# A top-k search tied to token tiles and matrix products, instead of running freely between two fixed pauses

## The chip, the cores and the metric

The kernel runs on one core of a Trainium2 chip. The metric is device time in microseconds (us) of one execution; lower is better. The engines named below are TensorE (PE; its weight loads are a row of their own, PEld), VectorE (DVE), ScalarE (ACT) and GpSimd (POOL); SyncE (SP) issues DMAs. Each engine works through its own instructions in one fixed order and waits at an instruction until its inputs and its buffers are ready.

## The reference, cut to what matters

The kernel computes one transformer layer for 1024 tokens of width 1024. The combined projection `h @ w_in` feeds an indexed sparse attention, a retention and two gates; then come an output projection and a gated feed-forward part.

```python
h = _rmsnorm(x, norm1_w) * (1.0 + scale1) + shift1
qa, ka, va, iq, ik, iw, qr, kr, vr, gr, ga, gb = split(h @ w_in)
# sparse attention: per query the 256 keys with the highest index score
score = einsum('bqh,bqhs->bqs', iw * w_scale, relu(einsum('bqhd,bsd->bqhs', iq, ik) * idx_scale))
_, idx = lax.top_k(where(causal, score, NEG), topk)
y_a = attention(qa, ka[idx], va[idx]) @ w_attn_proj
# retention: 4 heads, chunks of 128 tokens, a state r carried from chunk to chunk
ret = _retention(rotate(qr), rotate(kr), vr)
y_r = (silu(gr) * _head_groupnorm(ret, gn_w)) @ w_ret_proj
merged = sigmoid(ga) * y_a + sigmoid(gb) * y_r
```

## The kernel before

**Matrix products.** A float32 product is made of three passes on TensorE over operands split into a high and a low part (`whi`, `wlo`; `hT_hi`, `hT_lo`). ACT writes the high part of a weight (L77, L750), and the low part, the weight minus its high part, is a subtraction on POOL (L80, L751).

**Stages that the change touches, in order of time.** Times are of the profiled execution.
- About 128 to 238 us: the projection for the attention's values (`V`, 192 matmuls over 8 token tiles) with the index scores woven in. `score_units` makes the scores of query blocks 2 to 7 in units: four transposes (L414) and a split on DVE (`qst`, L417) per half of the heads, then per unit two matmuls (L424, L425), a ReLU on ACT (L428) and a multiply-add on DVE (L430, L432). A linear rule `n` of the step number says from which V step a unit comes after.
- 238 to 484 us: the retention in two pairs of heads (`hp` 0 and 1). Each pair has a Q/K projection with a rotation on POOL (L657), and then a loop over eight token tiles that makes V, the masked `inn` (a multiply on DVE, L675) and, one tile later, `chunk`: output, state `rst` (DVE, L694) and the statistics `bn_stats`, `bn_aggr` (DVE, L700, L701). During `hp` 0 `mod_work` computes the modulation vector from streamed weights (`macc`, DVE). During `hp` 1 `add_up` (L621, L623) forms `S1`, a sum of token halves of `h`; ScalarE and DVE split it (L633).
- 499 to 770 us: the gates and the attention's Q and K by a Strassen-like scheme: 13 streams of weight columns (`flow`), 7 products each (`M1` to `M7`, of 12 matmuls), 91 in all. The list `seq` sets their order; the first two streams alternate. `M5`, `M6`, `M3` and `M7` need the token sums `S1`, `S2`, `S4` and `S3`, which DVE forms and splits (L621, L623, L633); it also forms sums of weight blocks (`wraw`, L789, L796) and adds products (L810). `S3` is written over one of `h`'s own halves.
- 740 to 863 us: `make_g`, which transposes the gated retention, and `y_r`, its projection, whose results DVE multiplies (`sgr`, L1049). Attention starts behind it.

**The search.** `select_all` finds each query's 256th highest score without a sort. A first pass counts the scores that are not negative, 31 passes set one bit of the threshold each, and a last one counts what is strictly above: 33 passes of six counts on DVE (L464, over 384 to 1024 columns), each of the first 32 followed by two tiny instructions (`rej` L469, `cand` L484) that the next pass needs. A final select (L492 to L496) then writes the mask into the scores. The whole search has low priority (`LATE`): a scheduler, when the kernel is built, fills it in between DVE's other work. `turns_after(a, b)` adds only an order: `a` is placed behind `b`, without a semaphore. There are two such places: the pass of bit 8 stands behind the last split of `S3`, that of bit 3 behind the last `make_g`.

Of the kernel before, what the change touches and what calls it, by code (L numbers as in the profile page):

```python
# [15 lines left out]
ALU = mybir.AluOpType  # L16
# [27 lines left out]
def tile_hybrid_layer(ctx: ExitStack, tc: tile.TileContext, x, c, w_ada, b_ada, norm1_w, w_in,  # L44
# [395 lines left out]
    summed, loaded = [], []  # L440
    PAUSES = (8, 3)
    paused = []

# [6 lines left out]
    def select_all():  # L450
# [19 lines left out]


        for j, sc in enumerate(score):
            ins = nc.vector.tensor_scalar(eq[:, :sc.shape[1]], sc, 0.0, None, op0=ALU.is_ge, op1=ALU.add,
                                          accum_out=cnt[:, j:j + 1])
            tc.add_manual_dep(ins.ins, last_score[0].ins.name, NOSYNC, reason="scores first")
        rejected(-1)
        nc.vector.tensor_scalar(cand, rej, 1 << 30, None, op0=ALU.bitwise_xor)
        for bit in range(30, -1, -1):
            first = count(ALU.is_ge, at)
            if bit in PAUSES:  # L480
                paused.append(first)
            rejected(1 << bit)
            if bit:
                nc.vector.scalar_tensor_tensor(cand, cand, 1 << (bit - 1), rej, op0=ALU.bitwise_xor,  # L484
                                               op1=ALU.bitwise_xor)
            else:
                nc.vector.tensor_tensor(cand, cand, rej, op=ALU.bitwise_xor)
        count(ALU.is_gt, at)
        nc.vector.tensor_scalar(need, cnt, -1.0, float(TOPK), op0=ALU.mult, op1=ALU.add)
        for j, sc in enumerate(score):  # L490
            e, r = eq[:, :sc.shape[1]], rank[:, :sc.shape[1]]
            nc.vector.tensor_scalar(e, sc, at[j], None, op0=ALU.is_equal)  # L492
            nc.vector.tensor_tensor_scan(r, e, e, 0.0, op0=ALU.add, op1=ALU.max)
            nc.vector.scalar_tensor_tensor(e, r, need[:, j:j + 1], e, op0=ALU.is_gt, op1=ALU.mult)
            nc.vector.tensor_scalar(sc, sc, at[j], NEG, op0=ALU.is_lt, op1=ALU.mult)
            nc.vector.scalar_tensor_tensor(sc, e, NEG, sc, op0=ALU.mult, op1=ALU.add)  # L496
# [5 lines left out]
    ones = modp.tile([P, P], F32, name="ones")  # L502
    nc.vector.memset(ones, 1.0)

    def mod_work():
# [12 lines left out]
        for n, (m, k) in enumerate(steps):  # L518
# [8 lines left out]
            if behind is not None:  # L527
                turns_after(ins, behind)
            yield
            if k == KT - 1:  # L530
# [46 lines left out]
    for t in range(NT):  # L577
        ps = ps_mm()
        for k in range(KT):
            n = 5 * (KT * t + k) // 4 - 8  # L580
            while len(units) <= n and next(sgen, LATE) is not LATE:
                pass
            mm = mm_tok(ps, hT.lhs(t), slots, ks=(k,))
            if n >= 0:
                turns_after(mm, units[min(n, len(units) - 1)])
# [26 lines left out]
    def add_up(out, terms):  # L612

        first = True
        for name, k, sign in terms:
            for part in [out] if name is None else [f32(x[:, k, :]) for x in side[name]]:
                if first:
                    acc, s0, first = part, sign, False
                    continue
                if s0 > 0:  # L620
                    nc.vector.tensor_tensor(out, acc, part, op=ALU.add if sign > 0 else ALU.subtract)  # L621
                else:
                    nc.vector.tensor_tensor(out, part, acc, op=ALU.subtract)  # L623
                acc, s0 = out, 1

    def alloc_side(pl, name):
# [8 lines left out]
    for hp in range(2):  # L635
# [3 lines left out]
        for t in range(NT):  # L639
# [23 lines left out]
            if hp == 0:  # L663
                next(mgen, None)
        slots = [rows_slot([(w_in, C_VR + 2 * DV * hp, 2 * DV)], k) for k in range(KT)]
        r = [None, None]
        vs, inns = {}, {}

# [8 lines left out]
        def chunk(t, e, r):  # L677
# [22 lines left out]
            nc.vector.bn_stats(st6, on)  # L700
            nc.vector.bn_aggr(mv, st6)  # L701
            rs = rstd_of(retp, mv[:, 1:2], 1, 1.0, "g", nc.gpsimd)
# [6 lines left out]
        for t in range(NT + 1):  # L709
# [7 lines left out]
            if t:  # L717
                for e in range(2):
                    r[e] = chunk(t - 1, e, r[e])
            if hp == 0:  # L720
                next(mgen, None)
# [4 lines left out]
            elif 3 <= t < 7:  # L726
                k = t - 3
                add_up(sums[k], [("h12", k, 1), ("h22", k, 1)])
                split_sum("S1", k, sums[k])
# [143 lines left out]
    class GateEnv:  # L873
# [30 lines left out]
        def use(self, st, c):  # L904
# [14 lines left out]
            for e in range(2):  # L919
                h = 2 * (st.nt + nt) + e  # L920
                self.store(st, rot_d[:, which, h, :, cs], to[64 * e:64 * e + 16])
                for i, part in enumerate(parts):
                    nc.sync.dma_start(out=dst[h, 16:64, i, cs], in_=f32(part[64 * e + 16:64 * e + 64]))

    genv = GateEnv()
    flow = []
    for c0, func, dst, blocks in ((C_GR, AF.Silu, sgg_d, range(0, KT, 2)), (C_QA, None, (0, q_d), (0, 2)),
# [25 lines left out]
    for to, terms in (("S2", []), ("S4", [(None, -1), ("h21", 1)]), ("S3", [("h11", 1), ("h12", -1)])):  # L953
        for k in range(4):
            if terms:
                add_up(sums[k], [(n, k, sign) for n, sign in terms])
            split = split_sum(to, k, sums[k])
    turns_after(paused[0], split)

# [45 lines left out]
    n_mid = len(seq)  # L1005
    seq += [(st, m) for m in ("M1", "M2", "M5", "M6", "M7", "M4", "M3") for st in flow[-2:]]
    rope, staged = {}, {}

    def behind(i):
        n, m = 2 + (i - 14) // 7, seq[i][1]  # L1010
        if 14 <= i < n_mid:
            if m == "M1":
# [45 lines left out]
    for hf in range(2):  # L1058
        for nt in range(NF):
# [7 lines left out]
            else:  # L1067
                nc.sync.dma_start(out=m_d[nt], in_=sg)
    turns_after(paused[1], made)
    st_s.close()  # L1070
# [668 lines left out]
```

## Time and profile before

| what | value |
|---|---|
| median of 3 runs | 1787.7 us (1787.62 to 1791.78) |
| the profiled execution | 1787.85 us |
| its span in the trace | 1785.9 us (the rest, 2 us, lies around it) |
| mean granted TensorE clock | 0.989 of full speed |
| TensorE busy | 1701.2 us, 95% of the span |
| DVE, ACT, POOL busy | 1228.8, 754.3 and 888.6 us |

TensorE is busy for all but about 85 us of the span. A change that leaves the matmuls as they are can only win or lose in these idle times and in the clock.

### The profile page before, as it was taken

The numbers are of one execution on the slowest core, as the hardware profiler recorded it, in microseconds if no ns is written. First come the engines' busy times: TensorE is split into PE (matmuls) and PEld (weight loads), VectorE is DVE, ScalarE is ACT, GpSimd is POOL, SyncE is SP. The second block draws the span as 40 slices with busy tenths as digits, with TensorE's granted clock in tenths as the row PEclk, the third lists the DMA queues.
The fourth block names the chain that finished last, engine by engine and source line by source line (L and its number), as shares of the span: only waits on it lengthen the run. The fifth ranks groups of instructions, "written<-read, shape, count | busy, mean of one in ns | idle before, by whom it ended". The sixth has DMA issues, their size and how long they took to land. (4 is left out here: it accounts for less than half of the span.)

```text
span 1785.9 us, 24646 instructions
## 1 busy us (share of the span) xinstructions
PE 1701.2 (95%) x8266; PEld 1397.1 (78%) x8266; DVE 1228.8 (69%) x2089; ACT 754.3 (42%) x1469; POOL 888.6 (50%) x883
## 2 busy tenths in 40 slices
PE   5898989999989999999999999899999999999998
PEld 4797868787867888788777888688787878787887
DVE  7528789999699246469876656865656555686665
ACT  3625632342444344430477246533333333444444
POOL 4562275582665479530246640044444444556664
PEclk9999999999999999999999999999999999999999
DMA  9534552411423355865852740034445444597663
GB/s 291 147 108 144 159 161 54 148 33 51 127 77 112 116 156 186 257 203 161 193 128 72 249 162 1 30 118 159 144 151 178 147 137 147 187 311 259 212 185 109
DMA packets 182655, 266.49 MB, mean 149 GB/s; under 512 B 13872, under 2 KB 111616, under 8 KB 180096
## 3 DMA queue, kind: packets, MB, share of 16 engines
q1 hardware_dynamic: 182528, 264.91, 47.4%
q8 instruction: 65, 1.06, 0.2%
q14 instruction: 62, 0.51, 0.1%
HBM read 195.39 MB, written 69.47 MB: 148 GB/s over the span
## 5 line engine op out<-in xcount | busy, mean ns | idle before, releaser
L80 POOL TENSOR_TENSOR wlo<-wraw,whi 128x512 fp32r<-128x512 f32 (+2 forms) x116 | 144.7, 1261 | 111.4 <-ACT whi L77 101.0
L464 DVE TENSOR_SCALAR_CACHE_REDUCE eq<-score,cand 128x384 uint8<-128x384 f32 (+2 forms) x192 | 180.8, 942 | 4.5
L751 POOL TENSOR_TENSOR flo<-tmp,fhi 128x512 fp32r<-128x512 f32 x79 | 106.3, 1346 | 141.1 <-ACT fhi L750 77.0
L121 PE MATMUL mm<-whi,hT_hi 128*128 128x512 f32 (+1 forms) x432 | 160.2, 376 | 3.6 <-ACT qk L644 1.8
L123 PE MATMUL mm<-wlo,hT_hi 128*128 128x512 f32 (+1 forms) x432 | 161.5, 376 | 0.0
L124 PE MATMUL mm<-whi,hT_lo 128*128 128x512 f32 (+1 forms) x432 | 161.2, 376 | 0.0
L827 PE MATMUL ya<-hc,fhi 128*128 128x512 f32 x344 | 134.7, 392 | 2.3 <-DVE c L810 1.4
L1587 DVE TENSOR_TENSOR dslot<-draw,dslot 128x512 fp32r<-128x512 f32 x88 | 96.1, 1127 | 55.3 <-ACT dslot L1586 48.1
L829 PE MATMUL ya<-hc,fhi 128*128 128x512 f32 x344 | 134.1, 390 | 0.0
L1586 ACT ACTIVATE dslot<-draw 128x512 fp32r<-128x512 f32 x154 | 90.1, 626 | 102.1 <-DMA draw<-dw_d 22.8
L831 PE MATMUL ya<-hc,flo 128*128 128x512 f32 x344 | 132.5, 390 | 0.0
L1587 POOL TENSOR_TENSOR dslot<-draw,dslot 128x512 fp32r<-128x512 f32 x66 | 98.7, 1508 | 63.5 <-ACT dslot L1586 60.4
L751 POOL TENSOR_TENSOR flo<-raws,fhi 128x512 fp32r<-128x512 f32 x60 | 82.1, 1368 | 92.5 <-ACT fhi L750 64.3
L77 ACT ACTIVATE whi<-wraw 128x512 fp32r<-128x512 f32 (+2 forms) x116 | 67.0, 590 | 116.6 <-DMA wraw<-in_w_in_dram 48.4
L829 PE MATMUL yb<-hc,fhi 128*128 128x512 f32 x256 | 101.0, 395 | 6.1 <-DVE hc L1278 6.1
L831 PE MATMUL yb<-hc,flo 128*128 128x512 f32 x256 | 101.1, 395 | 3.2 <-POOL flo L751 3.2
L827 PE MATMUL yb<-hc,fhi 128*128 128x512 f32 x256 | 100.8, 395 | 0.6 <-DVE c L810 0.4
L750 ACT ACTIVATE fhi<-tmp 128x512 fp32r<-128x512 f32 x84 | 53.0, 631 | 113.3 <-PE ya L829 60.3
L751 POOL TENSOR_TENSOR wlo<-wraw,whi 128x512 fp32r<-128x512 f32 x52 | 80.5, 1556 | 35.1 <-ACT whi L750 33.3
L121 PEld LDWEIGHTS mm<-whi,hT_hi 128*128 128x128 f32 x432 | 81.2, 189 | 15.9 <-ACT qk L644 2.2
L1127 POOL TENSOR_SCALAR sx<-sx,mx 128x128 f32<-128x128 f32 (+7 forms) x64 | 47.5, 748 | 91.0 <-DVE mx L1126 69.4
L124 PEld LDWEIGHTS mm<-whi,hT_lo 128*128 128x128 f32 x432 | 81.7, 190 | 12.6 <-issue 0.5
(408 smaller groups left out, 4935.9 us busy)
## 6 DMA issues: line engine op xcount, KB each, us to landing
draw<-act_d SPq DMA_DIRECT2D x77, 256.0 KB
mw<-in_w_ada_dram SPq DMA_DIRECT2D x32, 512.0 KB
act_d<-c SPq DMA_DIRECT2D x64, 256.0 KB
raw<-in_w_in_dram SPq DMA_DIRECT2D x26, 512.0 KB
raws<-in_w_ffn_gate_dram SPq DMA_DIRECT2D x24, 512.0 KB
raws<-in_w_ffn_up_dram SPq DMA_DIRECT2D x24, 512.0 KB
dw<-in_w_ffn_down_dram SPq DMA_DIRECT2D x22, 512.0 KB
dw_d<-dw SPq DMA_DIRECT2D x11, 1024.0 KB
```

Of the source, the lines that this page charges most:

```text
L77: ins = nc.scalar.activation(hi[:, :n], raw[:, :n], AF.Copy)
L80: nc.gpsimd.tensor_sub(lo[:, :n], raw[:, :n], f32(hi[:, :n]))
L121: ins = nc.tensor.matmul(ps, lhsT=ahi, rhs=whi[:, :n], start=(i == 0), stop=False)
L123: nc.tensor.matmul(ps, lhsT=ahi, rhs=wlo[:, :n], start=False, stop=False)
L124: nc.tensor.matmul(ps, lhsT=alo, rhs=whi[:, :n], start=False, stop=(i == last))
L464: ins = [nc.vector.tensor_scalar(eq[:, :sc.shape[1]], sc, thr[j], None, op0=op, op1=ALU.add, accum_out=cnt[:, j:j + 1]) for j, sc in enume ...
L751: (eng or nc.gpsimd).tensor_sub(lo, src, f32(hi))
L827: mm = nc.tensor.matmul(ps, lhsT=whi[:, k, :], rhs=hhi[:, k, :], start=own and k == 0, stop=False, skip_group_check=True)
L829: nc.tensor.matmul(ps, lhsT=whi[:, k, :], rhs=hlo[:, k, :], start=False, stop=False, skip_group_check=True)
L831: nc.tensor.matmul(ps, lhsT=wlo[:, k, :], rhs=hhi[:, k, :], start=False, stop=k == 3, skip_group_check=True)
L1586: nc.scalar.activation(slot[:, 0], raw, AF.Copy)
L1587: lo_eng.tensor_sub(slot[:, 1], raw, f32(slot[:, 0]))
```

## The change

- The two pauses are gone. Instead the list `passes` holds the first count of all 33 passes and the first instruction of the final select, and `turns_after` ties: passes 1 to 3 behind the modulation work after token tiles 2, 4 and 6 of the first Q/K projection; passes 4 to 7 behind the statistics after tiles 2, 4, 6 and 8 of the first retention loop; passes 16 to 19 likewise in the second; passes 22 to 32 behind the sums of products 15, 21, and so on to 75; the final select behind the last `make_g`. Passes 8 to 15, 20 and 21 have no tie of their own.
- Score units start later in the V projection and come at 11/8 a step instead of 5/4.
- Each part of `S1` is tied to the statistics of its own token tile, so that its sums stand spread over the loop.
- Until product 6 is prepared, the low parts of the product weights are computed on DVE (new line L762) instead of POOL: ten of them.
- The last two streams run `M1`, `M2` of one, then of the other, and only then alternate.

```diff
-    PAUSES = (8, 3)
-    paused = []
+    passes = []
...
+        passes.append(None)
...
         for bit in range(30, -1, -1):
             first = count(ALU.is_ge, at)
-            if bit in PAUSES:
-                paused.append(first)
+            passes.append(first)
             rejected(1 << bit)
...
-        count(ALU.is_gt, at)
+        passes.append(count(ALU.is_gt, at))
...
-            nc.vector.tensor_scalar(e, sc, at[j], None, op0=ALU.is_equal)
+            ins = nc.vector.tensor_scalar(e, sc, at[j], None, op0=ALU.is_equal)
+            if j == 0:
+                passes.append(ins)
...
+            mod_ins[0] = ins
...
-            n = 5 * (KT * t + k) // 4 - 8
+            n = 11 * (KT * t + k) // 8 - 16
...
     def add_up(out, terms):
 
-        first = True
+        acc = ins = None
         for name, k, sign in terms:
             for part in [out] if name is None else [f32(x[:, k, :]) for x in side[name]]:
-                if first:
-                    acc, s0, first = part, sign, False
+                if acc is None:
+                    acc, s0 = part, sign
                     continue
                 if s0 > 0:
-                    nc.vector.tensor_tensor(out, acc, part, op=ALU.add if sign > 0 else ALU.subtract)
+                    step = nc.vector.tensor_tensor(out, acc, part, op=ALU.add if sign > 0 else ALU.subtract)
                 else:
-                    nc.vector.tensor_tensor(out, part, acc, op=ALU.subtract)
+                    step = nc.vector.tensor_tensor(out, part, acc, op=ALU.subtract)
+                ins = ins or step
                 acc, s0 = out, 1
+        return ins
...
                 next(mgen, None)
+                if t in (2, 4, 6):
+                    turns_after(passes[t // 2], mod_ins[0])
...
-            nc.vector.bn_aggr(mv, st6)
+            chunked[0] = nc.vector.bn_aggr(mv, st6)
...
+            if t and t % 2 == 0:
+                turns_after(passes[(3, 15)[hp] + t // 2], chunked[0])
...
-                add_up(sums[k], [("h12", k, 1), ("h22", k, 1)])
+                turns_after(add_up(sums[k], [("h12", k, 1), ("h22", k, 1)]), chunked[0])
                 split_sum("S1", k, sums[k])
                 add_up(sums[k], [(None, k, 1), ("h11", k, -1)])
...
+    genv.lo_engine = nc.vector
...
-            split = split_sum(to, k, sums[k])
-    turns_after(paused[0], split)
+            split_sum(to, k, sums[k])
...
-    seq += [(st, m) for m in ("M1", "M2", "M5", "M6", "M7", "M4", "M3") for st in flow[-2:]]
+    seq += [(st, m) for st in flow[-2:] for m in ("M1", "M2")]
+    seq += [(st, m) for m in ("M5", "M6", "M7", "M4", "M3") for st in flow[-2:]]
...
+        if i == 6:
+            genv.lo_engine = None
+        if i >= 15 and (i - 15) % 6 == 0 and 22 + (i - 15) // 6 < len(passes) - 1:
+            turns_after(passes[22 + (i - 15) // 6], genv.added)
...
-    turns_after(paused[1], made)
+    turns_after(passes[-1], made)
```

Line numbers move: in the changed kernel the counts are L463, `rej` and `cand` L468 and L483, `inn` L683, the statistics L708 and L709, sums L625 and L627, their splits L639, weight sums L800 and L807, product sums L821, `sgr` L1066.

TensorE where the index scores start; `mm` is the V projection, `tr` the transposes of the scores' queries, `lg` the scores. Before:

```order
L414 MATMUL tr<-ident,iqd 128x128 x4
L123 MATMUL mm<-wlo,hT_hi_119 128x512
L124 MATMUL mm<-whi,hT_lo_120 128x512
L121 MATMUL mm<-whi,hT_hi_119 128x512
L123 MATMUL mm<-wlo,hT_hi_119 128x512
L124 MATMUL mm<-whi,hT_lo_120 128x512
L121 MATMUL mm<-whi,hT_hi_119 128x512
L123 MATMUL mm<-wlo,hT_hi_119 128x512
L124 MATMUL mm<-whi,hT_lo_120 128x512
L121 MATMUL mm<-whi,hT_hi_119 128x512
L424 MATMUL lg<-khi,qst 128x384
L425 MATMUL lg<-klo,qst 128x384
```

And in the changed kernel:

```order
L414 MATMUL tr<-ident,iqd 128x128 x4
L123 MATMUL mm<-wlo,hT_hi_119 128x512
L124 MATMUL mm<-whi,hT_lo_120 128x512
L121 MATMUL mm<-whi,hT_hi_119 128x512
L123 MATMUL mm<-wlo,hT_hi_119 128x512
L124 MATMUL mm<-whi,hT_lo_120 128x512
L121 MATMUL mm<-whi,hT_hi_119 128x512
L123 MATMUL mm<-wlo,hT_hi_119 128x512
L124 MATMUL mm<-whi,hT_lo_120 128x512
L414 MATMUL tr<-ident,iqd 128x128 x4
L424 MATMUL lg<-khi,qst 128x384
L425 MATMUL lg<-klo,qst 128x384
```

The first transposes now come behind 28 matmuls of V instead of 10, and the second four come ahead of the first score: 36 matmuls and 8 transposes stand ahead of it, where there were 19 and 4.

DVE where `S1` begins, in the second retention loop. Before:

```order
L464 TENSOR_SCALAR eq,cnt<-score_769,cand 128x512
L621 TENSOR_TENSOR sums<-hT_hi_121,hT_lo_122 128x512 x4
L464 TENSOR_SCALAR eq,cnt<-score_770,cand 128x640
L621 TENSOR_TENSOR sums<-sums,hT_hi_121 128x512 x4
L464 TENSOR_SCALAR eq,cnt<-score_771,cand 128x768
L675 TENSOR_TENSOR inn<-tr,rmask 128x128
L621 TENSOR_TENSOR sums<-sums,hT_lo_122 128x512 x4
L464 TENSOR_SCALAR eq,cnt<-score_772,cand 128x896
```

And in the changed kernel, in the middle of the same loop:

```order
L709 BN_AGGR mv<-st_4645 128x2
L625 TENSOR_TENSOR sums<-hT_hi_121,hT_lo_122 128x512
L463 TENSOR_SCALAR eq,cnt<-score_768,cand 128x384
L625 TENSOR_TENSOR sums<-sums,hT_hi_121 128x512
L683 TENSOR_TENSOR inn<-tr,rmask 128x128
L708 BN_STATS st_4708<-on 128x6
L463 TENSOR_SCALAR eq,cnt<-score_769,cand 128x512
L625 TENSOR_TENSOR sums<-sums,hT_lo_122 128x512
L683 TENSOR_TENSOR inn<-tr,rmask 128x128
```

The sums stood four and four ahead of an `inn`; now one by one between the steps of the loop, with the passes 15 to 18 among them.

DVE after the last statistics of the retention, ahead of the first products (`raw` and `wraw` are weight blocks and their sums, `S_5192` is `S2`). Before:

```order
L701 BN_AGGR mv<-st_4931 128x2
L796 TENSOR_TENSOR wraw<-raw_4948 128x512
L796 TENSOR_TENSOR wraw<-raw_4947,wraw 128x512
L796 TENSOR_TENSOR wraw<-raw_4945,wraw 128x512
L633 TENSOR_TENSOR S_5192<-sums,S_5192 128x512 x2
L796 TENSOR_TENSOR wraw<-raw_4947,raw_4946 128x512
L623 TENSOR_TENSOR sums<-hT_hi_119,sums 128x512
```

And in the changed kernel:

```order
L709 BN_AGGR mv<-st_4931 128x2
L463 TENSOR_SCALAR eq,cnt<-score_768,cand 128x384
L807 TENSOR_TENSOR wraw<-raw_4948 128x512
L807 TENSOR_TENSOR wraw<-raw_4947,wraw 128x512
L463 TENSOR_SCALAR eq,cnt<-score_769,cand 128x512
L762 TENSOR_TENSOR wlo<-raw_4948,whi 128x512
L762 TENSOR_TENSOR wlo<-wraw,whi 128x512
L463 TENSOR_SCALAR eq,cnt<-score_770,cand 128x640
L762 TENSOR_TENSOR wlo<-wraw,whi 128x512 x2
```

Between the last statistics and the last split of `S3` DVE had 43 subtractions and additions of 128x512; now it has 53, nine of them low parts, and ten counts.

## Rows read from the trace of the kernel before

**Rows 1.** The page's busy times of each engine, shares of the span.

```profile
PE 1701.2 (95%) x8266; PEld 1397.1 (78%) x8266; DVE 1228.8 (69%) x2089; ACT 754.3 (42%) x1469; POOL 888.6 (50%) x883
```

**Rows 2.** TensorE's timeline: start, duration, instruction, [idle ahead <- released by].

```profile
141.62 0.69 PE L424 MATMUL lg<-khi,qst 128*128 128x384 f32 x1 [4.47 <-DVE qst L417]
...
298.31 0.38 PE L673 MATMUL tr<-qkT 128*128 128x128 f32 x1 [1.18 <-DVE inn L675]
...
425.31 0.49 PE L673 MATMUL tr<-qkT 128*128 128x128 f32 x2 [2.16 <-DVE inn L675]
...
511.57 0.50 PE L827 MATMUL mm<-S,whi 128*128 128x512 f32 x1 [1.33 <-ACT kept L807]
...
522.79 0.50 PE L827 MATMUL lg<-S,whi 128*128 128x512 f32 x1 [2.75 <-ACT kept L807]
...
529.33 0.50 PE L829 MATMUL mm<-hT_lo,whi 128*128 128x512 f32 x1 [0.99 <-DVE hT_lo L633]
532.21 0.50 PE L829 MATMUL mm<-hT_lo,whi 128*128 128x512 f32 x1 [1.23 <-DVE hT_lo L633]
...
566.15 0.50 PE L827 MATMUL mm<-hT_hi,whi 128*128 128x512 f32 x1 [3.27 <-ACT kept L807]
...
728.15 0.50 PE L827 MATMUL mm<-hT_hi,whi 128*128 128x512 f32 x1 [2.51 <-DVE sums L810]
...
863.39 0.39 PE L1115 MATMUL lga<-kk,qs 128*128 128x256 f32 x1 [2.50 <-DVE sgr L1049]
```

**Rows 3.** Windows: length, busy us of PE, PEld, DVE, ACT, POOL; granted clock, DMA.

```profile
298.00:365.00 67.00, 63.08 (x299) 51.77 (x300) 62.72 (x159) 21.97 (x51) 33.01 (x59) 1.00 0.35 105
365.00:422.00 57.00, 57.00 (x268) 47.15 (x267) 55.05 (x111) 19.13 (x47) 41.89 (x62) 1.00 0.17 45
422.00:484.00 62.00, 59.75 (x279) 49.99 (x279) 48.68 (x131) 25.50 (x52) 28.67 (x55) 1.00 0.31 92
...
533.00:600.00 67.00, 62.69 (x275) 51.31 (x274) 49.55 (x91) 23.42 (x42) 24.20 (x18) 1.00 0.32 103
600.00:740.00 140.00, 137.43 (x597) 112.81 (x597) 65.42 (x56) 63.23 (x112) 112.85 (x81) 0.99 0.56 171
```

**Rows 4.** Windows of 10 us with a lowered granted clock, same columns.

```profile
140.00:150.00 10.00, 8.02 (x33) 6.78 (x34) 6.26 (x13) 4.22 (x8) 2.62 (x5) 0.83 0.43 138
...
520.00:530.00 10.00, 6.26 (x20) 4.66 (x20) 10.00 (x14) 5.17 (x10) 3.45 (x3) 0.83 0.18 54
...
860.00:870.00 10.00, 7.43 (x35) 5.66 (x34) 9.10 (x39) 5.49 (x18) 2.26 (x5) 0.83 0.86 238
```

**Rows 5.** The counts' group on the page: busy us, mean ns, idle before.

```profile
L464 DVE TENSOR_SCALAR_CACHE_REDUCE eq<-score,cand 128x384 uint8<-128x384 f32 (+2 forms) x192 | 180.8, 942 | 4.5
```

**Rows 6.** DVE's timeline, a long `rej` and four sums ahead of `inn`.

```profile
284.20 5.86 DVE L469 TENSOR_SCALAR rej<-cnt 128x6 int32<-128x6 f32 x1
...
421.62 2.50 DVE L621 TENSOR_TENSOR sums<-sums,hT_hi 128x512 f32<-128x512 f32 x4
```

**Rows 7.** DVE's timeline from the last statistics to the last `S3` split.

```profile
485.78 0.18 DVE L701 BATCH_NORM_AGGREGATE mv<-st 128x2 f32<-128x6 f32 x1
...
500.41 1.78 DVE L633 TENSOR_TENSOR S<-sums,S 128x512 fp32r<-128x512 f32 x1
502.11 0.68 DVE L623 TENSOR_TENSOR sums<-hT_hi,sums 128x512 f32<-128x512 f32 x1
...
530.40 1.76 DVE L633 TENSOR_TENSOR hT_lo<-sums,hT_hi 128x512 fp32r<-128x512 f32 x1
```

**Rows 8.** POOL's timeline, two low parts among the first products.

```profile
499.90 1.74 POOL L751 TENSOR_TENSOR wlo<-wraw,whi 128x512 fp32r<-128x512 f32 x1
509.55 4.03 POOL L751 TENSOR_TENSOR wlo<-wraw,whi 128x512 fp32r<-128x512 f32 x1 [7.91 <-ACT whi L750]
```

**Rows 9.** DVE's timeline, the final select's end.

```profile
861.51 1.23 DVE L496 SCALAR_TENSOR_TENSOR score<-eq,score 128x1024 f32<-128x1024 uint8 x1
862.65 0.68 DVE L1049 TENSOR_TENSOR sgr<-mm,sgr 128x512 f32<-128x512 f32 x1
```

More of the change, by code (lines that the diff above doesn't have):

```diff
@@ L503, in tile_hybrid_layer @@
     nc.vector.memset(ones, 1.0)
+    mod_ins = [None]
     def mod_work():
@@ L664, in tile_hybrid_layer @@
                 next(mgen, None)
+                if t in (2, 4, 6):
+                    turns_after(passes[t // 2], mod_ins[0])
         slots = [rows_slot([(w_in, C_VR + 2 * DV * hp, 2 * DV)], k) for k in range(KT)]
         r = [None, None]
-        vs, inns = {}, {}
+        vs, inns, chunked = {}, {}, [None]
         def inner(t, e):
```

## The prediction, as it was put on record

> **What bounds the kernel now.** I read the page first: TensorE is busy for 1701.2 of 1785.9 us, DVE for 1228.8 [rows 1]. So TensorE is the bound, and what this change can touch is the 85 us in which it stands still, and the clock. Next I read TensorE's timeline for the idle time ahead of single matmuls, between the index scores and the start of attention, the stretch in which the diff moves anything. The ten gaps of [rows 2] make 22.4 us. The reader is to see who ends them, seven times DVE and three times an ACT copy, and where they lie: at the first index scores (4.47 us), at the start of the first retention loop (1.18) and of the second (2.16), four among the first products, one early in the steady products (3.27), one at their end (2.51), one ahead of attention (2.50).
>
> The windows tell why. In the first retention loop DVE is busy for 62.7 of 67 us, as full as TensorE, in the Q/K projection behind it for 55.1 of 57; then for only 48.7 of 62, and for 65.4 of 140 in the late products [rows 3]. The search is what fills it: 192 counts of 0.942 us, 180.8 us [rows 5], so a pass is 6 × 0.942 = 5.7 us and two tiny instructions, some 6 us. The work sits where DVE is full, while it idles later. Three 10 us windows run at a granted clock of 0.83 of full speed, each around one of these gaps [rows 4]: at 140, 520 and 860. At 2.4 GHz outside and a mixture with 1.2 GHz inside, each costs 10 × 0.17 = 1.7 us beside its gap.
>
> **Index scores, 128 to 238 us.** TensorE waits 4.47 us at 141.62 for the first split of the queries on DVE [rows 2]. The change puts 17 more matmuls of V and 4 more transposes ahead of the first score. In the window 365 to 422, where TensorE never idles, one instruction takes 57.00 / 268 = 0.213 us [rows 3], so these 21 are 4.5 us of cover: as much as the gap. The second half's split must now be ready at about the same time, so I leave 1.5 us of it. Gain 3.0, and the 1.7 of the clock: **4.7**. Bounds: nothing, if the units, now 10% denser, make TensorE wait later in the same stage instead; 6.2 if all of it goes.
>
> **First retention loop, 298 to 365.** Six passes ran here, three run after. That is 18 counts and their small instructions less, 18 us: DVE falls from 62.7 to about 45 of 67 us. TensorE idles for 67.0 − 63.1 = 3.9 us of the window, and 0.9 of the wait at its start lies ahead of it: 4.8. The second loop, with DVE at 48.7 of 62, idles for 2.25, and 2.16 of that is the wait that the four-and-four sums cause [rows 2, 3]. I take **4.2**; bounds 0 and 4.8. The three passes do not vanish: each must run before the products. Passes 1 to 3 are held back behind the modulation work in 246 to 298, where a `rej` once stood for 5.86 us [rows 6]; nothing on TensorE waits for the search there, so this costs nothing by itself.
>
> **Q/K projection and second loop, 365 to 484.** In the projection there is one pass more (6) and the eight sums ahead of the loop go (two groups as the 2.50 us one [rows 6]): 55.1 + 6.0 − 5.0 = 56 of 57, nothing. In the loop DVE gets those 5.0 us and some five counts (4.7) more: 48.7 + 9.7, about 59 of 62, that is 95%. The first loop at 94% lost 4.2 to 4.8; I take 4.0, where 2.16 is lost now: **−1.8**. Queued behind each count or sum are `inn` and `rst`, and TensorE waits for both. Bounds: +2.2, if single sums of 0.6 never hold up an `inn` as a group of 2.50 did; −12, if POOL's nine low parts of this stage each meet a sum at 1.10 us (the next part has this price).
>
> **First products, 484 to 533.** DVE needs 46.4 us from the last statistics (485.78) to the last split of `S3` (530.40 + 1.76 = 532.16) [rows 7]; TensorE loses 1.33 + 2.75 + 0.99 + 1.23 = 6.3 us in the meantime, and 1.7 by the clock [rows 2, 4]. Alone a 128x512 subtraction has a pitch of 0.60 us (its row says 0.68, the next starts 0.60 later), and 1.78 when a POOL low part lies beside it: 1.10 more [rows 7, 8]. After: 53 of these × 0.60 = 31.8, ten counts 9.4, together 41.2 us. Ten of POOL's 17 low parts are gone from here; seven stay, at most 7 × 1.10 = 7.7. Half of that makes 45.0, 1.4 us earlier than now. Besides, 72 instead of 64 matmuls of the gate are left for TensorE behind the loop, 8 × 0.213 = 1.7 us more cover. Gain **3.0**. Bounds: 8.0 if all goes; −9 if all seven meet and a low part on DVE waits for its high part, as POOL's did for 7.91 us [rows 8], with `S3` queued behind it.
>
> **The Trainium skill** (SBUF — State Buffer, "Who interferes with whom") speaks against this part: a VectorE instruction with two SBUF inputs contends with a GpSimd instruction that reads SBUF, and the one that starts second blocks for the whole of the first. By that rule a meeting would cost the full 1.74 us of the POOL row [rows 8], and the seven 12.2 us instead of 7.7. The trace agrees that they collide, but the row shows 1.10 more, so the sum goes by 1.10.
>
> **Products from 533 to 770.** Passes 22 to 32 come one per six products instead of five in a row between 533 and 578. DVE was at 49.6 of 67 us there; three passes instead of five leave it at 38. The wait of 3.27 us at 566 stands among those five; I take **2.5**, bounds −3 and 4.3 (TensorE idles for 67.0 − 62.7 = 4.3 in that window). In 600 to 740 DVE is at 65.4 of 140, so some seven more passes, 42 us, find room. The wait of 2.51 at 728 is for a product sum queued behind a weight sum; that order stands as before: **0**, bounds −2 and 4.2.
>
> **Start of attention.** The final select runs to 862.7, and the last `sgr` multiplications queue behind it, so attention's first matmul comes at 863.39, 2.50 us after the last `y_r` matmul (860.89) [rows 2, 9]. After, passes 28 to 32 are done earlier, so the select begins right behind `make_g` and ends earlier; the last eight `sgr` stand behind it. What is left is two of 0.68: gain 1.2, and 1.7 by the clock [rows 4]: **2.9**, bounds 0 and 4.2.
>
> **The sum.** 4.7 + 4.2 − 1.8 + 3.0 + 2.5 + 0 + 2.9 = 15.5. From the profiled execution's 1787.85 that is 1772.4; the median is 0.15 below that execution, so I predict **1772 us**, 0.9% faster. The low bounds together (0, 0, −12, −9, −3, −2, 0) are 26 us slower, the high ones (6.2, 4.8, 2.2, 8.0, 4.3, 4.2, 4.2) 34 faster; they will not all come together.
>
> **Rivals.**
> - *The waits move instead of going.* For: the same 22 passes stand ahead of the products, so DVE's work from 246 to 533 is not less, only spread; and V has no more matmuls, so what covers the first scores is missing later. Then the scores gain nothing, the loop pays 4 instead of 1.8, the first products gain nothing: 4.2 − 4.0 + 2.5 + 2.9 = 5.6, 1782. Against: DVE idles for 13 of 62 us in the second loop's window and for 17 of 67 behind 533 [rows 3], so there is room to spread into.
> - *More goes.* The first products lose nothing (8.0) and the wait at 728, with the lowered clock around it, goes (4.2): 1772 − 5.0 − 4.2 = 1763. For: seven passes of relief around 533 to 580. Against: nothing in the order at 728 changes.
> - *DVE becomes the bound from 424 to 533* (slower). Place: the queue of sums, counts and the new low parts. If all nine POOL low parts of the second loop and all seven of the products meet two-input work, that adds 9 × 1.10 + 3.8 to my sum, and one low part that waits 7.9 us for ACT [rows 8] adds that: 21.6, less the 3 us that DVE has free in the loop, and two more 10 us windows at 0.83 clock, 3.4: 1772 + 22 = 1794. It makes the kernel slower once it adds over 21 us. Against: the sums are single instructions of 0.60 us, spread over 60 us, so that all sixteen must be met is unlikely.
>
>   By the Trainium skill's whole blocking (same page and section) each of the 16 meetings would cost up to 0.64 us more than by the row, and this rival would give 1804; no run here shows it yet.
>
> **How the numbers follow.** No change can be told within about 0.3%, 5.4 us. Forecast 0.48 (1765 to 1779), the waits move 0.22 (half of it below 1782), more goes 0.17, DVE the bound 0.13 (some of it ends below 1793). Faster: 0.48 + 0.17 + 0.11 = 0.76; same 0.11 + 0.03 = 0.14; slower 0.10. The range goes from below the second rival to beyond the first: 1759 to 1787. The forecast's own is 1765 to 1779.
>
> **What would show it.** Right: the gap ahead of the first score below 2 us and a clock near 1.00 at 140 to 150; no wait over 1 us in the first loop; `S3`'s last split about 45 us behind the last statistics; no wait over 2 us around 566; attention's first matmul about 1.3 us behind the last `y_r` matmul. Wrong: waits of 2 us and more for `inn` or `rst` in the second loop; low parts on DVE (L762) with idle time ahead that ACT ends, and `S3` more than 46 us behind the statistics; a count ahead of a product sum on which TensorE waits.

## The result, and the profile after

The changed kernel takes 1768.47 us (median of 4 runs, 1763.71 to 1772.03), the one before 1787.66 us: a ratio of 0.9888, 95% interval 0.9857 to 0.992, so 1.1% faster. The forecast was 1772 us, range 1759 to 1787. The profiled execution took 1770.31 us, with a span of 1768.4.

The page, same lines as [rows 1] and [rows 5]: TensorE does its work with 5 us less busy time, the counts cost the same.

```profile
PE 1696.3 (96%) x8266; PEld 1393.6 (79%) x8266; DVE 1216.7 (69%) x2099; ACT 757.2 (43%) x1469; POOL 882.4 (50%) x873
...
L463 DVE TENSOR_SCALAR_CACHE_REDUCE eq<-score,cand 128x384 uint8<-128x384 f32 (+2 forms) x192 | 180.5, 940 | 3.6
```

TensorE's timeline, the longer waits between the index scores and attention, to hold against [rows 2]. The reader is to see that the wait of 4.47 at the first scores, those of the loops but one of 0.82, the 3.27 behind 533 and the 2.50 at attention's start are gone; new are 0.84, 1.14 and 1.78 in the scores, one for a POOL rotation at 251, 3.54 for `S3` at 517 and 1.25 for an ACT copy at 677. Waits that both kernels have (1.8 for `qk` at 234, and 1.6 and 1.7 for two rotations behind 257) are left out.

```profile
146.48 0.63 PE L414 MATMUL tr<-ident,iqd 128*128 128x128 f32 x4 [0.84 <-DVE iqd L411]
165.04 0.39 PE L424 MATMUL lg<-khi,qst 128*128 128x256 f32 x1 [1.14 <-ACT rl L428]
187.63 0.39 PE L424 MATMUL lg<-khi,qst 128*128 128x256 f32 x1 [1.78 <-DVE gateb L565]
251.64 0.33 PE L667 MATMUL tr<-ident,kk 128*128 128x128 f32 x1 [1.07 <-POOL kk L663]
465.73 0.70 PE L696 MATMUL lg<-vs,kk 128*128 128x256 f32 x2 [0.82 <-ACT on L705]
517.61 0.50 PE L838 MATMUL mm<-hT_hi,whi 128*128 128x512 f32 x1 [3.54 <-ACT hT_hi L638]
527.35 0.50 PE L840 MATMUL mm<-hT_lo,whi 128*128 128x512 f32 x1 [0.69 <-DVE hT_lo L639]
677.48 0.50 PE L838 MATMUL lg<-S,whi 128*128 128x512 f32 x1 [1.25 <-ACT kept L818]
711.61 0.50 PE L838 MATMUL mm<-hT_hi,whi 128*128 128x512 f32 x1 [1.88 <-DVE sums L821]
864.40 0.36 PE L1132 MATMUL lga<-kk,qs 128*128 128x256 f32 x1 [0.61 <-DMA kk<-k_d]
```

Its windows, as [rows 3] and [rows 4]. TensorE no longer stands still in 298 to 365 and in 533 to 600; DVE fell from 62.7 to 52.6 us in the first loop's window, rose to 53.7 in the second's and from 65.4 to 108.0 in the late products. The granted clock, 0.83 at 140 before, is 1.00; over 484 to 533 it is 0.97 as before. The last line is that window in the kernel before.

```profile
140.00:150.00 10.00, 9.06 (x45) 7.12 (x44) 8.20 (x12) 5.76 (x13) 2.48 (x3) 1.00 0.65 218
...
298.00:365.00 67.00, 67.00 (x324) 56.57 (x323) 52.61 (x130) 26.28 (x59) 40.56 (x74) 1.00 0.38 111
...
422.00:484.00 62.00, 61.18 (x283) 51.14 (x282) 53.70 (x129) 28.32 (x57) 32.36 (x50) 1.00 0.37 108
484.00:533.00 49.00, 44.77 (x188) 35.93 (x187) 49.00 (x72) 22.91 (x40) 21.68 (x12) 0.97 0.30 91
533.00:600.00 67.00, 67.00 (x297) 55.48 (x297) 48.69 (x96) 26.95 (x48) 30.08 (x23) 1.00 0.37 117
600.00:740.00 140.00, 136.87 (x605) 112.49 (x604) 108.03 (x159) 64.07 (x113) 106.74 (x78) 0.99 0.62 190
```

```profile
484.00:533.00 49.00, 42.70 (x177) 33.93 (x176) 42.86 (x48) 22.86 (x41) 30.57 (x20) 0.97 0.29 89
```

**Where the time came from.** Since the matmuls are the same in both kernels, their work can be counted along TensorE's timeline: add up the moving columns of every matmul (3,560,368 in each kernel), and read at which time each kernel reaches the same sum. The difference is the lead of a kernel over the one before, in one execution each. The left column is the time in the kernel before.

| at, us | changed | e1 no ties | e2 old scores | e3 low on POOL | e5 rej form | e8 S3 first | e9 double pass | e11 low to ten |
|---|---|---|---|---|---|---|---|---|
| 128 | -0.4 | 1.1 | -0.1 | -0.6 | -0.5 | 0.7 | 0.0 | 0.1 |
| 240 | 2.4 | 3.0 | -0.2 | 5.1 | -2.1 | 5.2 | 3.1 | 2.8 |
| 285 | 1.1 | 1.8 | -0.1 | 2.9 | -2.2 | 3.1 | -0.8 | 2.0 |
| 365 | 7.7 | 8.4 | 6.5 | 9.5 | -2.1 | 9.1 | 5.7 | 8.6 |
| 422 | 7.1 | 1.7 | 4.8 | 8.0 | -2.1 | 7.6 | -0.6 | 7.0 |
| 499 | 9.3 | 2.1 | 5.8 | 8.7 | -3.5 | 9.0 | -0.1 | 8.4 |
| 546 | 11.8 | 8.9 | 6.7 | 7.1 | -3.3 | 8.8 | 2.7 | 13.1 |
| 610 | 16.9 | 10.0 | 11.8 | 12.2 | -3.2 | 13.6 | 5.1 | 18.2 |
| 770 | 16.3 | 10.2 | 12.3 | 12.7 | -3.2 | 12.9 | 6.9 | 17.2 |
| 900 | 18.1 | 9.8 | 13.8 | 14.6 | -3.3 | 11.8 | 7.1 | 19.0 |

Each column is one execution, and a small difference between two of them shows little. e5 runs its instructions in the order of the kernel before and still falls 3.5 us behind. Eleven kernels here have the new interleave of the scores; their gain from 128 to 240 runs from -0.3 us (e6) to 6.0 (e3). Much of that is the clock: over 128 to 240 it was granted at 0.97 in e6, 0.98 in the changed kernel and 1.00 in e3, and each hundredth is 1.1 us of that stretch.

### The profile page after: what moved, and what is told of

The parts are those of the page before. It is cut to its first block, busy times and chain, and to the rows that moved or that the text cites. A ratio compares the mean times of both kernels' runs of the same rounds, so it can differ in the third digit from the quotient of the medians.

```text
span 1768.4 us, 24625 instructions
## 1 busy us (share of the span) xinstructions
PE 1696.3 (96%) x8266; PEld 1393.6 (79%) x8266; DVE 1216.7 (69%) x2099; ACT 757.2 (43%) x1469; POOL 882.4 (50%) x873
## 5 line engine op out<-in xcount | busy, mean ns | idle before, releaser
L463 DVE TENSOR_SCALAR_CACHE_REDUCE eq<-score,cand 128x384 uint8<-128x384 f32 (+2 forms) x192 | 180.5, 940 | 3.6
L762 POOL TENSOR_TENSOR flo<-tmp,fhi 128x512 fp32r<-128x512 f32 x79 | 107.1, 1356 | 139.7 <-ACT fhi L761 111.8
L1604 POOL TENSOR_TENSOR dslot<-draw,dslot 128x512 fp32r<-128x512 f32 x66 | 98.0, 1498 | 65.4 <-ACT dslot L1603 61.7
L762 POOL TENSOR_TENSOR flo<-raws,fhi 128x512 fp32r<-128x512 f32 x60 | 82.1, 1369 | 92.7 <-ACT fhi L761 64.2
L124 PEld LDWEIGHTS mm<-whi,hT_lo 128*128 128x128 f32 x432 | 81.3, 189 | 12.7 <-issue 0.5
L807 DVE TENSOR_TENSOR tmp<-raws 128x512 f32<-128x512 f32 x40 | 39.5, 989 | 74.3 <-POOL flo L762 74.3
```

The costliest lines, as they stand in the source:

```text
L124: nc.tensor.matmul(ps, lhsT=alo, rhs=whi[:, :n], start=False, stop=(i == last))
L463: ins = [nc.vector.tensor_scalar(eq[:, :sc.shape[1]], sc, thr[j], None, op0=op, op1=ALU.add, accum_out=cnt[:, j:j + 1]) for j, sc in enume ...
L762: (eng or nc.gpsimd).tensor_sub(lo, src, f32(hi))
L1604: lo_eng.tensor_sub(slot[:, 1], raw, f32(slot[:, 0]))
```

## The experiments

Medians of each, with its interval as a ratio to runs of the kernel before on the same chip (1787.5 to 1788.2 us).

**e1: the changed kernel without ties.**

```diff
-                if t in (2, 4, 6):
-                    turns_after(passes[t // 2], mod_ins[0])
...
-            if t and t % 2 == 0:
-                turns_after(passes[(3, 15)[hp] + t // 2], chunked[0])
...
-            split_sum(to, k, sums[k])
+            split = split_sum(to, k, sums[k])
+    turns_after(passes[23], split)
...
-        if i >= 15 and (i - 15) % 6 == 0 and 22 + (i - 15) // 6 < len(passes) - 1:
-            turns_after(passes[22 + (i - 15) // 6], genv.added)
...
-    turns_after(passes[-1], made)
+    turns_after(passes[28], made)
```

> The changed kernel, but the search's passes have no ties again, only the two old pauses (bit 8 behind the last split of S3, bit 3 behind the last make_g). Theory (the search was in DVE's way where DVE was full): passes 6 to 11 stand in the first retention loop again, so TensorE loses 5 to 7 us there; five passes in a row stand behind 533 and cost about 4; the final select holds up the start of attention by 2.5 us. Against that no pass stands among the first products, so the last split of S3 comes some 10 us earlier and 3 to 4 us of waiting for it go. Net 7 to 9 us slower than the changed kernel, about 1776. Rival (the ties only shift the waits, the gain is in the sums, the scores and the low parts): within 2 us of the changed kernel.

1778.2 us, ratio 0.9938 (0.9921 to 0.9955): some 10 us slower than the changed kernel, so the ties are half of the gain. But not where the theory put it. TensorE loses nothing in the first loop, although DVE is as full as before; the window of this kernel:

```profile
298.00:365.00 67.00, 67.00 (x325) 56.53 (x323) 63.91 (x159) 26.85 (x61) 40.88 (x74) 1.00 0.38 111
```

What it loses lies at the start of the second loop, 7 us between 400 and 422. There a `rej` was held for 6.27 us, and the `inn` that TensorE waits for came late behind it and the passes; DVE's row, then TensorE's:

```profile
395.84 6.27 DVE L468 TENSOR_SCALAR rej<-cnt 128x6 int32<-128x6 f32 x1
```

```profile
414.85 0.79 PE L679 MATMUL tr<-qkT 128*128 128x128 f32 x2 [3.31 <-DVE inn L681]
```

Of the 7 us, 3.3 are this wait and some 3.5 the clock around it, granted at 0.84 over the 22 us:

```profile
400.00:422.00 22.00, 18.69 (x75) 15.14 (x75) 21.26 (x49) 1.58 (x3) 2.08 (x4) 0.84 0.11 27
```

The hold alone does not do this. In e3 a `rej` is held for the same 6.27 us at 394.77, ten counts stand between it and `inn` where e1 has twelve, and TensorE waits 0.58 us.

Behind 499 the forecast of the theory holds: without passes among them the first products gain 6.8 against 2.5 up to 546; up to 610 this kernel gains 1.1, the changed one 5.1; and attention's start waits 2.50 us for `sgr`, as before.

**e2: old interleave of the scores.** One line: `n = 5 * (KT * t + k) // 4 - 8`.

> The changed kernel with the old interleave of index scores and V projection (5/4 a step, from 8 steps). Theory (late start covers the first split): the wait of about 4.5 us and the lowered clock (0.83 for 10 us, 1.7) return, the later waits in this stage (1.1 and 1.8 us in the changed kernel) shrink: about 3 us slower, 1771. Rival (the waits only move within the stage): the lead at the end of the scores stays the same within 1 us.

1770.52 us, ratio 0.9896 (0.9881 to 0.9911), 2 us slower by medians, which can't be told from none. The old wait is back, and the clock at 140 to 150 is 0.83 again:

```profile
141.86 0.54 PE L424 MATMUL lg<-khi,qst 128*128 128x384 f32 x1 [4.32 <-DVE qst L417]
```

The lead from 128 to 240 is 0 instead of 2.8. But from 240 to 285 this kernel loses nothing, and the changed kernel, e3 and e8 lose 1.3, 2.2 and 2.1: POOL's rotation does not come earlier along with TensorE. So both theory and rival hold in part, one after the other. What the new interleave is worth is not shown: at 285 the eleven kernels that have it lead by -1.2 (e6) to 4.1 us (e7), and e2 with -0.1 lies among them.

**e3: low parts on POOL.** `genv.lo_engine = nc.vector` and its end at product 6 left out.

> The changed kernel with the ten low parts of the first products on GpSimd again. Theory by the row (a meeting of a GpSimd low part with two-input work on DVE costs DVE 1.10 us): DVE saves 10 x 0.6 = 6 and pays up to 10 x 1.1 = 11, so the last split of S3 comes up to 5 us later and the kernel is 1 to 4 us slower. By whole blocking (1.74 a meeting) it would be up to 11 us later, 6 to 10 us slower. Rival (DVE's queue is the bound there, and each low part on it only lengthens it): S3 about 6 us earlier, 2 to 4 us faster.

1775.16 us, ratio 0.9926 (0.9913 to 0.994): 6.7 us slower by medians, though the interval still touches the changed kernel's. In the profiles 4.0 of it lie between 499 and 546. `S3`'s last split comes 53.8 us behind the last statistics, 51.8 in the changed kernel, and TensorE waits longer for it, 4.35 against 3.54 us, and 1.44 for `S` before that; the clock over 484 to 533 was 0.93 against 0.97:

```profile
519.03 0.80 PE L838 MATMUL mm<-hT_hi,whi 128*128 128x512 f32 x1 [4.35 <-ACT hT_hi L638]
```

DVE has six tenths of a us less for each of ten low parts, some 2 us more of counts in the stretch (twelve for ten), and still ends later instead of 6 us earlier: the rival falls. Between 420 and 535, DVE's 128x512 rows of two inputs last over 1.2 us 15 times here, 10 times in the changed kernel. The stretch fits the row's price, the median the whole blocking (the profiled execution is the fastest of its six, 1771.83 us); this does not decide between the two.

**e4 and e7, e10: sums untied; the old order of the last streams; both.**

```diff
-                turns_after(add_up(sums[k], [("h12", k, 1), ("h22", k, 1)]), chunked[0])
+                add_up(sums[k], [("h12", k, 1), ("h22", k, 1)])
```

> The changed kernel with S1's sums untied, so that ten of them stand in a row ahead of an inn at the start of the second retention loop. Theory (a group of sums holds up inn): TensorE waits there 4 to 6 us, since a sum takes 0.6; DVE then has less to do later in the loop, so the end of the loop may win 1 back: 3 to 5 us slower, about 1772. Rival (the loop has slack, TensorE has other matmuls to run meanwhile): within 1 us.

> The changed kernel with the old order of the last two streams (M1, M1, M2, M2). The prediction gave this part nothing. Theory: within 1.5 us of the changed kernel, the wait of 1.9 us for a product sum near 711 becomes the 2.4 to 2.5 us of before. Rival (the new order gives the sum 2.7 us more cover): 2 us slower.

> The changed kernel without two of its parts, the ties of S1's sums and the new order of the last two streams, each of which alone changed the time by less than 1 us. Theory: they are worth nothing together as well, within 1.5 us of the changed kernel. Rival (each covers for the other): 3 us slower.

1768.68 us (0.9889, 0.9874 to 0.9903), 1769.22 us (0.9904, 0.9885 to 0.9923) and 1769.37 us (0.9899, 0.9869 to 0.9928): none differs from the changed kernel. The wait for `inn` with ten sums ahead of it was 0.86 us, not 4 to 6: DVE came to them early enough that `inn` was hardly late. Two parts of the change are worth nothing that can be measured here.

**e5 and e6: another form of `rej`**, in the kernel before and in the changed one. `step` is a new table of the bits' values, filled by POOL ahead of the search.

```diff
-            nc.vector.tensor_scalar(rej, cnt, float(TOPK), float(value), op0=ALU.is_lt, op1=ALU.mult)
+            nc.vector.scalar_tensor_tensor(rej, cnt, float(TOPK), step[:, i:i + 1].to_broadcast([P, n]),
+                                           op0=ALU.is_lt, op1=ALU.mult)
```

> The kernel before, with the order untouched, but rej computed by another form of instruction: scalar_tensor_tensor with the bit's value from a small table, where it was tensor_scalar with the value as a constant. In the kernel before a rej of 0.17 us took 5.86 us at 284 and again at 404, each time until GpSimd's run of instructions for one token tile had ended, while cand, which is a scalar_tensor_tensor, never took over 1.3 us. Theory (these holds, not the number of passes in the loop, made the first retention loop wait): no rej over 1.5 us, TensorE loses at most 1 us in the first loop instead of 5 to 6, and less at 425: 6 to 8 us faster than before, about 1780. Rival (the six passes fill DVE, the hold costs nothing): the first loop loses 4 us or more as before, time within 2 us of 1787.

> The changed kernel with the same form of rej. Its profiled run showed no hold over 1.3 us, though its neighbours with nearly the same order showed one of 4.6 to 6.3 us at 395 to 400. Theory (a hold comes or not by a few tenths of a us of timing): the median falls by 0 to 2 us, and the runs, which spread over 8 us, lie closer together. Rival (the spread is from elsewhere): median and spread unchanged.

1785.45 us (0.9992, 0.9978 to 1.0006) and 1768.79 us (0.9902, 0.9882 to 0.9922): nothing. The holds did not go, so what they cost was not tested; the form is not what makes them. In e5 both stand where they stood, and its lead stays flat through the first loop:

```profile
286.39 5.86 DVE L474 SCALAR_TENSOR_TENSOR rej<-cnt,step 128x6 int32<-128x6 f32 x1
```

**e8: pass 20 behind `S3`.**

```diff
-            split_sum(to, k, sums[k])
+            split = split_sum(to, k, sums[k])
+    turns_after(passes[20], split)
```

> The changed kernel with one tie more: pass 20 stands behind the last split of S3, so that six to ten counts less (5 to 9 us) stand among the sums on which the first products wait. Theory (there DVE is the bound, busy for 49.0 of 49 us): S3's last split comes 5 to 9 us earlier, the waits of 3.5 and 0.7 us and the lowered clock there go, 3 to 5 us faster, about 1765; the passes find room later, where DVE idles. Rival (the wait only moves to the product sums behind): within 1 us.

1774.18 us, ratio 0.9928 (0.991 to 0.9946), 5.7 us slower by medians (the interval still touches the changed kernel's): the theory was wrong. The last split came 49.3 us behind the statistics, not 43 to 47. Without counts between them, DVE's two-input instructions ran from 503.74 to 511.04 without a pause, and one low part of POOL, 1.30 us alone, took 8.43 us beside them; then DVE stood still for 2.43 us until low parts were done, and three sums met the next ones and took 5.12 us. POOL, then DVE:

```profile
503.76 8.43 POOL L762 TENSOR_TENSOR wlo<-raw,whi 128x512 fp32r<-128x512 f32 x1
```

```profile
513.47 1.76 DVE L807 TENSOR_TENSOR wraw<-raw,wraw 128x512 f32<-128x512 f32 x1 [2.43 <-POOL wlo L762]
...
516.84 5.12 DVE L625 TENSOR_TENSOR sums<-sums,hT_lo 128x512 f32<-128x512 f32 x3
```

TensorE waited 5.13 us in one piece:

```profile
523.21 0.80 PE L840 MATMUL mm<-hT_lo,whi 128*128 128x512 f32 x1 [5.13 <-DVE hT_lo L639]
```

Not all of the loss is from here: this profile also has waits of 1.35 us at 745 and 1.99 at 869 for a DMA, where the changed kernel has none and 0.61, and from 770 to 900 it loses 1.1 where that one gains 1.8.

**e9: e1 with one pass counted twice**, at bit 27 (the second count repeats the first).

```diff
             first = count(ALU.is_ge, at)
             passes.append(first)
+            if bit == 27:
+                count(ALU.is_ge, at)
             rejected(1 << bit)
```

> The kernel without ties of the first experiment, whose first retention loop cost nothing although DVE was busy for 63.9 of 67 us there, with the six counts of the pass of bit 27 done twice: 5.7 us more for DVE some 10 us ahead of the loop, the length of the hold that rej met there in the kernel before, and nothing else. Theory (the hold, a backlog of 5.9 us that DVE carries into a loop which fills it, is what the first loop paid for in the kernel before): the waits for inn, rst and the ACT copy come back, 4 to 6 us lost between 290 and 365 against the kernel without ties. Rival (the loop's waits come from the order of the passes in it): it loses less than 1.5 us.

1775.17 us, ratio 0.9939 (0.9911 to 0.9966). The first loop lost nothing (from -0.8 at 285 to 5.7 at 365), with DVE at 64.5 of 67 us. By the letter this speaks for the rival, but the backlog did not arrive: the order was made anew with it, the first `inn` stands three counts into pass 5 where e1 has three counts into pass 6, and it ran at 292.44; in the kernel before it ran at 297.97, just ahead of the wait that ended at 298.31 [rows 2]. The test is inconclusive.

**e11 and e12: low parts on DVE until product 10**; in e12 with pass 20 behind `S3` as well. The edit: `if i == 10:` for `if i == 6:`.

> The changed kernel with the low parts on DVE until product 10 is prepared, where it was 6: four more of them. Theory by the rows (a low part costs DVE 0.6 us; the GpSimd one costs it 1.1 to 1.2 us if it meets a sum, and in the changed kernel ten of these met): S3's last split about 2 us earlier, 1 to 2 us faster. Rival (DVE's length is all that counts): 2 us slower.

> The changed kernel with both: low parts on DVE until product 10, and pass 20 behind the last split of S3. With pass 20 alone the sums, with no counts among them, met GpSimd's low parts (three sums took 5.12 us) and S3 came only 2 us earlier. Theory (without those meetings the counts' 6 to 9 us come out): S3's last split 5 us or more earlier than in the changed kernel, the wait there below 1 us, 2 to 4 us faster. Rival (the PE order of the first products, not DVE's length, is what costs): within 2 us or slower.

1767.69 us (0.9892, 0.9863 to 0.9922) and 1768.65 us (0.9894, 0.9864 to 0.9924). In the profile e11 gains 4.7 between 499 and 546 where the changed kernel gains 2.5; `S3`'s last split comes 51.1 us behind the statistics, 0.7 earlier and not 2, and 0.8 us of a median can't be told from none. e12 is 5.5 us faster than e8 by medians but does not beat the changed kernel: the time is that of its rival. Its last split comes 49.8 us behind the statistics, no earlier than e8's, and one low part of POOL took 11.31 us (507.78 to 519.09). So that the meetings with POOL cost e8 its time is not shown; e12 differs from it in TensorE's waits there (0.62, 1.93 and 0.72 us against 0.86 and 5.13), and by about 3 us behind 770.

## Why the prediction held, step by step

The sum was 15.5 us, the profiled spans differ by 17.5 and the medians by 19.2. That it came so near is in part luck: by the table four stretches gave 4.8 us less than forecast and three 7.8 more. Term by term, from the leads (the changed kernel was 0.4 behind at 128):

| stretch | forecast | measured | what the runs say |
|---|---|---|---|
| scores, 128 to 240 | 4.7 | 2.8 | wait and clock right (e2), size not shown |
| Q/K, 240 to 285 | 0 | -1.3 | missed |
| first loop, 285 to 365 | 4.2 | 6.6 | size near, reason wrong (e1) |
| to the first product, 365 to 499 | -1.8 | 1.6 | wrong sign |
| first products, 499 to 546 | 3.0 | 2.5 | size near by errors that cancel |
| products, 546 to 770 | 2.5 | 4.5 | right (e1), larger |
| attention's start, 770 to 900 | 2.9 | 1.8 | right (e1), smaller |

*Scores.* The 21 instructions of cover did what was said: the first wait went and the clock stayed at 1.00 there. The wait term was mis-sized: TensorE's waits of over 0.35 us from 128 to 230 fell from 5.5 to 3.8 us, 1.7 and not 3.0. New waits of 1.14 and 1.78 in the same stage are the rival "the waits move" in part, and the 1.3 lost to POOL's rotation is more of it: a bound that the prediction did not look at, since its waits were outside the moved work. POOL is busy for 47.2 of 50 us from 240 to 290.

*First loop.* The step that failed is "the work sits where DVE is full": DVE was at 63.9 and 64.5 of 67 us in e1 and e9, and TensorE waited for nothing. Nor did 18 counts leave the window: 35 stood in it before and 26 after, and DVE fell to 52.6, not to 45. The gain of 6.6 lies beyond the bound of 4.8.

The prediction saw the `rej` of 5.86 us ahead of the loop [rows 6] and said that such a hold "costs nothing by itself". The trace shows what it did: behind it DVE works without a pause up to the first `inn`. TensorE had made the input of that one by 291.80; it ran 6.2 us later, of which other matmuls covered some 5 and TensorE waited 1.18. In e1, whose loop is as full, it ran at once. TensorE and DVE of the kernel before, then of e1:

```profile
291.41 0.39 PE L673 MATMUL tr<-qkT 128*128 128x128 f32 x2
...
297.97 0.29 DVE L675 TENSOR_TENSOR inn<-tr,rmask 128x128 f32<-128x128 f32 x1
```

```profile
289.35 0.39 PE L679 MATMUL tr<-qkT 128*128 128x128 f32 x2
...
289.77 0.29 DVE L681 TENSOR_TENSOR inn<-tr,rmask 128x128 f32<-128x128 f32 x1
```

The two kernels that have this hold ahead of the loop (the one before, and e5, with an `inn` as late) wait in it. In the twelve others the first `inn` ran at once and none waits more than 0.4 us in the window, with 24 to 29 counts in it or 38 and 39. At the start of the second loop seven kernels with a hold of 4.6 to 6.3 us have an `inn` that is 5.1 to 5.2 us late; DVE is busy there for only 54 to 56 of 62 us, and they lose 1.4 to 1.6 us up to 422. So the likely cause is a backlog from the hold that a full loop can't work off. The backlog is shown; that it alone made TensorE wait is argued, since e5 did not remove the hold and e9 did not set up the backlog. The changed kernel has no count in that place: passes 4 to 6 wait for the statistics of the loop. e1 (without the ties) and e2 (with the old interleave) escaped the hold too.

*To the first product.* "I take 4.0" was worked out by likeness to the first loop's 94%, the reading that e1 refuted. DVE was at 53.7 of 62 us, and the sums met POOL's low parts there (these took up to 1.75 us) at no cost to TensorE.

*First products.* The size came out by two errors. `S3`'s last split was put 45 us behind the last statistics; it came after 51.8 (477.25 to 529.00), later than before, and beyond the 46 that the prediction had named as a sign of being wrong. The term that failed is "half of that" for the meetings: eleven of POOL's low parts fell into the stretch, not seven, and DVE's rows in it are 9.2 us longer than alone, where the sum had 3.85; another 1.5 us DVE was idle. The second error is the clock, whose 1.7 us did not come back (0.97 in both kernels). DVE rows of the changed kernel; the second is two meetings with POOL at the price of [rows 7]:

```profile
477.25 0.18 DVE L709 BATCH_NORM_AGGREGATE mv<-st 128x2 f32<-128x6 f32 x1
...
511.55 3.47 DVE L625 TENSOR_TENSOR sums<-sums,hT_hi 128x512 f32<-128x512 f32 x2
...
528.15 0.85 DVE L639 TENSOR_TENSOR hT_lo<-sums,hT_hi 128x512 fp32r<-128x512 f32 x1
```

It cost TensorE 3.54 + 0.69 us in place of four waits of 6.3, probably because `S2` and `S4` came early, without POOL beside them until 501.72. I had priced the whole chain by its end.

*Products and attention.* One pass per six products cleared the wait at 566 and, with it, more: a second one of 1.04 at 576, and 5.1 in all by 610. At 711 the wait stayed (1.88), as said. The prediction took 863.39 for attention's first matmul; four of attention's matmuls had run from 860.26 to 860.89, and the wait of 2.50 was that of the fifth. In the changed kernel the select's last instruction starts at 811.36, far ahead of the last `sgr` at 844.52, and nothing is left of this wait, where 1.3 had been forecast. Waits of 0.58 and 0.61 for POOL and a DMA at 848 and 864, inside attention, are new, and the stretch gained less than forecast.

*The rival of DVE as the bound* came halfway: DVE was busy for all of 484 to 533. Of DVE's 128x512 rows from 420 to 535, ten lasted over 1.2 us, three in the loop and seven behind it; the rival had sixteen meetings. No low part on DVE waited 7.9 us for ACT. By **the Trainium skill** (SBUF — State Buffer, "Who interferes with whom") the loser of a meeting blocks for the whole of one instruction; the two sums at 511.55 beside low parts of 1.7 us agree with that (1.74 each), as well as with 0.60 and 1.10: a low part that meets nothing takes 1.30 us (kernel before, 288.74), so the 1.74 of its row already hold some wait of its own.

## What to carry to other kernels

Low-priority work that fills an engine costs by what it stands ahead of and, it seems, by the backlog that it enters a stage with, not by the busy share of a window: the same loop ran free with DVE at 63.9 of 67 us. When work is moved between two engines that collide, count the meetings: ten subtractions of 0.6 us on the busier engine were cheaper here than on the idle one. A part of a change that covers a wait pays only as far as the next bound; look which engine stands behind it.

## What the runs showed of the hardware

A tiny DVE instruction that starts while POOL works was let in at the end of that one POOL instruction in some cases, and only at the end of POOL's whole unbroken run in others. In the kernel before, `rej` at 284.20 ended at 290.06 [rows 6], when the last of seven POOL instructions that followed without a pause had ended (290.04); in e9 one took 10.02 us, over eleven. In the changed kernel one got in after 1.28 us. DVE and POOL rows of e9, then of the changed kernel:

```profile
394.77 10.02 DVE L468 TENSOR_SCALAR rej<-cnt 128x6 int32<-128x6 f32 x1
...
404.27 0.48 POOL L665 TENSOR_TENSOR kk<-rra,rrb 128x128 f32<-128x128 f32 x1
```

```profile
389.31 1.28 DVE L468 TENSOR_SCALAR rej<-cnt 128x6 int32<-128x6 f32 x1
...
390.51 0.47 POOL L662 TENSOR_TENSOR rq<-rra,rrb 128x128 f32<-128x128 f32 x1
```

The counts of up to 1024 columns beside the same POOL work keep their time (1.28 us at 387.98 as elsewhere), and both forms of `rej` that were tried are held (5.86 us in e5). It goes the other way round as well: a low part of POOL that began beside an unbroken run of DVE's two-input work took 4.03 us in the kernel before [rows 8], 8.43 in e8 and 11.31 in e12, where it takes 1.30 alone. What decides between the short and the long hold stays open.
